# Hymba decoder step on one core: tiles 6 and 7 of the PEER layer gather u and v rows side by side

## The chip, the cores and the metric

The kernel runs on one core of a Trainium2 chip. The metric is the device time of one execution in microseconds; 3248.42 us is the median of three runs of the kernel before, which lie between 3223.76 and 3261.47 us.

## What is computed

One step of a hybrid decoder layer on 1056 tokens (1024 of a prompt, 8 x 4 sampled ones) of width 1024: an RMSNorm, a token mixer (windowed attention, gated linear attention, retention), a second RMSNorm, a PEER feed-forward layer, a final RMSNorm. The change lies in the PEER layer. It picks, for each token, 8 x 16 = 128 of 16384 experts, each of which is one row of `u_tab` and one of `v_tab` (1024 floats each):

```python
eidx = ...            # (tokens, 128): the chosen experts of each token
gate = softmax(...)   # (tokens, 128)
u = take(u_tab, eidx); v = take(v_tab, eidx)
pre = einsum('td,ted->te', xb, u)
act = gelu(pre, approximate=False) * gate
y   = x + einsum('te,ted->td', act, v)
```

## The kernel before

The tokens are cut into nine tiles of 128 rows (tile 8 has the 32 sampled tokens). The mixer runs over groups of tiles (0; 1, 2; 3, 4; 5, 8; 6, 7). Behind a tile's mixer its experts are selected on VectorE (the select ends with L710, which writes the expert numbers `ei`), and its PEER layer is done in one of two ways.

**Dense**, for tiles 2 to 5 together (512 tokens, `dense()`). All 16384 experts are gone through in 128 blocks of 128. The gates have been scattered into a dense matrix `gsd` in HBM, from which SP loads 2 MB pieces `Gt`. For block e, `up(e)` loads 512 KB of `in_uT` and 512 KB of `in_v_tab` on SP's queue into `raw` (four buffers), splits each into a high part on ScalarE (`uh`, `vh`, L981) and a low part on GpSimd (`ul`, `vl`, L982), and makes 24 matmuls of 128x512 into one PSUM bank `pre` (L1008): hh with uh, hl with uh, hh with ul. `hh` and `hl` are the high and low part of the four tiles' normed rows and are made once at the start. Then ScalarE takes the Gelu in place (L1009), VectorE multiplies by `Gt` (L1012), and the result is split into `ah` (ScalarE) and `al` (VectorE, L982). For each four blocks, `down` makes 8 groups of 12 matmuls into `out` banks (L1024), each of which VectorE adds to `oT` (L1028). At the end the four tiles are transposed back, normed and stored (L1053, L884).

**Gather**, for tiles 0, 1, 8, 6, 7 in this order (`gather()`). For each of the 128 expert columns GpSimd starts an indirect DMA that brings 128 rows of `u_tab`, one for each token, 512 KB, into one of six buffers `g` (L915). VectorE multiplies the buffer with the normed rows h2 and sums along the row in one instruction (L917, an STT below, with a short read of the accumulator behind it). After all 128 columns one Gelu (L919) and one multiply by the gates follow, and a second round of 128 indirect DMAs brings rows of `v_tab` (L930), which VectorE scales and adds to `gacc` (L932). `final` (L882 to L885) norms and stores the tile. For tiles 6 and 7 (`PSG`), h2 and then the sum lie one after the other in one PSUM tile `gacc` of two banks; PSUM's other banks are three of `pre` and three of `out`.

The order of each engine's instructions is fixed when the program is built, by a scheduler that goes by priorities: the dense path stands above the gathers, and the gathers come in where they fit. Each engine then works strictly in this order, so an instruction that waits holds up all behind it.

## Time and profile before

| | us | share of the span |
|---|---|---|
| median of three runs | 3248.42 | |
| the profiled execution, whole | 3220.93 | |
| its span, first to last instruction | 3219.0 | |
| TensorE busy | 2883.6 | 90% |
| VectorE busy | 2379.4 | 74% |
| GpSimd busy | 1897.8 | 59% |
| ScalarE busy | 1182.8 | 37% |
| moved by DMA | 980.51 MB, 305 GB/s | |

The time of all runs is the device time of one execution; the profile is of one more execution, whose span leaves out some 2 us around the program. Busy time is a mean over very different stretches: the mixer until about 1700 us, and behind it the dense path with the gathers of tiles 6 and 7 beside it. So it is read stretch by stretch. A wait is put down in the trace to the instruction or the DMA that ended it. A matmul's time as listed overlaps the next one's; the number of matmuls in a stretch gives their pace.

### The profile page before, as it was taken

The page shows a single profiled execution, that of the slowest core. Times are in us where ns is not written, and L with a number is a line of the kernel's source. Part 1 is how long each engine was busy: PE and PEld are TensorE (multiplying, and loading weights), DVE is VectorE, ACT ScalarE, POOL GpSimd, SP SyncE. Part 2 cuts the span into 40 slices and gives each one's busy share as a digit, 9 for nine tenths or more (in the row PEclk, how much of TensorE's full clock was granted, in tenths as well). Part 3 has the DMA queues.
Part 4 walks back from the last instruction along what each step waited for, and adds up shares of the span by engine and source line. Part 5 has one row for each costly group of instructions (what it writes and reads, how often), then busy time and mean ns, then how long its engine had stood idle before and what let it go on. Part 6 is the DMA issues. An engine that isn't in the chain of part 4 may idle for free. (4 is left out here: it accounts for less than half of the span.)

```text
span 3219.0 us, 41048 instructions
## 1 busy us (share of the span) xinstructions
PE 2883.6 (90%) x13566; PEld 2318.1 (72%) x13566; DVE 2379.4 (74%) x5398; ACT 1182.8 (37%) x2478; POOL 1897.8 (59%) x1447
## 2 busy tenths in 40 slices
PE   6887999996999899986764699999999999999997
PEld 5675777774786567775653578888888888888886
DVE  0375777999799967989989866667776676666673
ACT  1211213322575266776673322232323223222331
POOL 0026655655445434435554777777777888777782
PEclk9798889998899999978866899999999999999998
DMA  6379898999898988979898899999999999999982
GB/s 229 127 256 362 321 339 321 358 337 347 290 355 321 337 314 305 340 272 350 275 324 245 277 316 317 307 320 323 321 325 312 316 316 333 317 317 311 318 326 86
DMA packets 421541, 980.51 MB, mean 305 GB/s; under 512 B 163841, under 2 KB 193042, under 8 KB 421330
## 3 DMA queue, kind: packets, MB, share of 16 engines
q0 software_dynamic: 159808, 580.62, 49.5%
q1 hardware_dynamic: 261522, 397.28, 38.1%
q8 instruction: 107, 1.75, 0.2%
q14 instruction: 104, 0.85, 0.1%
HBM read 925.91 MB, written 51.45 MB: 304 GB/s over the span
## 5 line engine op out<-in xcount | busy, mean ns | idle before, releaser
L915 POOL DMA_INDIRECT g<-in_u_tab,ei x512 | 566.1, 1106 | 464.5 <-DVE g L917 187.1
L930 POOL DMA_INDIRECT g<-in_v_tab,ei x512 | 569.8, 1113 | 435.3 <-DVE gacc L932 136.1
L917 DVE SCALAR_TENSOR_TENSOR g<-g,gacc 128x1024 f32<-128x1024 f32 x544 | 654.0, 1216 | 133.3 <-DMA g<-in_u_tab,ei 125.0
L932 DVE SCALAR_TENSOR_TENSOR gacc<-g,pre,gacc 128x1024 f32<-128x1024 f32 x544 | 697.5, 1282 | 54.4 <-DMA g<-in_v_tab,ei 51.0
L1024 PE MATMUL out<-ah,vh 128*128 128x512 f32 x1024 | 385.4, 391 | 42.5 <-ACT vh L981 42.4
L1024 PE MATMUL out<-ah,vl 128*128 128x512 f32 x1024 | 392.8, 390 | 6.7 <-POOL vl L982 6.7
L1024 PE MATMUL out<-al,vh 128*128 128x512 f32 x1024 | 396.8, 391 | 0.3
L982 POOL TENSOR_TENSOR ul<-raw,uh 128x1024 fp32r<-128x1024 f32 x128 | 308.0, 2407 | 46.0 <-ACT uh L981 39.8
L982 POOL TENSOR_TENSOR vl<-raw,vh 128x1024 fp32r<-128x1024 f32 x128 | 306.8, 2413 | 10.5 <-ACT vh L981 9.2
L1028 DVE TENSOR_TENSOR oT<-oT,out 128x512 f32<-128x512 f32 x248 | 166.5, 684 | 144.5 <-PE out L1024 143.8
L1008 PE MATMUL pre<-hh,uh 128*128 128x512 f32 x1024 | 258.5, 394 | 16.2 <-DVE al L982 15.0
L1008 PE MATMUL pre<-hh,ul 128*128 128x512 f32 x1024 | 257.7, 394 | 12.6 <-POOL ul L982 12.6
L630 PE MATMUL pj<-hT,w 128*128 128x256 f32 (+2 forms) x1280 | 258.2, 352 | 4.6 <-ACT hT L261 2.8
L1008 PE MATMUL pre<-hl,uh 128*128 128x512 f32 x1024 | 258.3, 389 | 0.0
L1024 PEld LDWEIGHTS out<-ah,vh 128*128 128x128 f32 x1024 | 192.9, 189 | 83.8 <-ACT vh L981 42.8
L963 PE MATMUL sct<-o,o 128*128 128x128 f32 x1024 | 200.2, 334 | 58.7 <-ACT st L964 19.8
L981 ACT ACTIVATE uh<-raw 128x1024 fp32r<-128x1024 f32 x128 | 135.4, 1058 | 311.0 <-DMA raw<-in_uT 306.0
L1009 ACT ACTIVATE pre<-pre 128x512 f32<-128x512 f32 x128 | 74.5, 582 | 476.0 <-PE pre L1008 475.8
L963 PEld LDWEIGHTS sct<-o,o 128*128 128x128 f32 x1024 | 166.7, 229 | 99.7 <-ACT st L964 34.9
L1008 PEld LDWEIGHTS pre<-hh,uh 128*128 128x128 f32 x1024 | 194.4, 190 | 58.5 <-DVE al L982 15.4
L1008 PEld LDWEIGHTS pre<-hh,ul 128*128 128x128 f32 x1024 | 193.0, 190 | 57.8 <-POOL ul L982 18.0
L630 PEld LDWEIGHTS pj<-hT,w 128*128 128x128 f32 x1280 | 213.1, 197 | 28.6 <-issue 4.6
(293 smaller groups left out, 4874.6 us busy)
## 6 DMA issues: line engine op xcount, KB each, us to landing
raw<-in_uT SPq DMA_DIRECT2D x128, 512.0 KB, 4.5
raw<-in_v_tab SPq DMA_DIRECT2D x128, 512.0 KB, 5.2
w<-in_w_pqT SPq DMA_DIRECT2D x80, 512.0 KB, 6.4
gsd<-st SPq DMA_DIRECT2D x64, 512.0 KB, 6.4
Gt<-gsd SPq DMA_DIRECT2D x16, 2048.0 KB, 22.5
w<-in_w_inT SPq DMA_DIRECT2D x60, 512.0 KB, 6.7
w<-in_w_nat SPq DMA_DIRECT2D x60, 512.0 KB, 5.4
w<-in_w_outc SPq DMA_DIRECT2D x40, 512.0 KB, 7.1
```

The costliest lines, as they stand in the source:

```text
L630: PE.matmul(p[:, :T], w[:, kt, :], h2T[:, kt], start=kt == 0, stop=kt == 7)
L915: G.indirect_dma_start(out=g, out_offset=None, in_=I["u_tab"], in_offset=bass.IndirectOffsetOnAxis(ap=idx[:, e:e + 1], axis=0))
L917: V.scalar_tensor_tensor(g, g, 1.0, h2, op0=OP.mult, op1=OP.mult, accum_out=pre[:, e:e + 1])
L930: G.indirect_dma_start(out=g, out_offset=None, in_=I["v_tab"], in_offset=bass.IndirectOffsetOnAxis(ap=idx[:, e:e + 1], axis=0))
L932: V.scalar_tensor_tensor(acc, g, act[:, e:e + 1], acc, op0=OP.mult, op1=OP.add)
L963: PE.matmul(p[:, k * 128:(k + 1) * 128], o2[:, k % 2], o1, start=True, stop=True)
L981: S.activation(hi, x, AF.Copy)
L982: eng.tensor_tensor(lo, x, f(hi), op=OP.subtract)
L1008: PE.matmul(p, w[:, kt], x[:, kt], start=kt + n == 0, stop=kt == 7 and n == 2)
L1009: S.activation(p, p, AF.Gelu)
L1024: PE.matmul(p, w[:, ds], x, start=j + n == 0, stop=j == EG - 1 and n == 2)
L1028: V.tensor_tensor(oT[:, dt], oT[:, dt], p, op=OP.add)
```

## The change

Tiles 6 and 7 get a function of their own, `gather_rows()`. A new input `uv_tab` holds each expert's row of `u_tab` and its row of `v_tab` side by side, 8 KB. For each expert column one indirect DMA brings 128 such rows, 1 MB, into one of three buffers `g2` (8 KB a partition each; before there were six of 4 KB). VectorE forms the sum with h2 on the left half, ScalarE takes the Gelu of this one column and multiplies it by the gate (two instructions of 128x1), and VectorE adds the scaled right half to `gacc`. So there are 256 indirect DMAs for the two tiles instead of 512, and one pass instead of two. h2 and the sum lie in PSUM at the same time (`gh2`, `gacc`, two banks each); for this `pre` and `out` get two banks each instead of three. The pool `gat` of the other gathers is closed with the mixer's pools, and the gathers of tiles 0, 1 and 8 are issued ahead of that; `hl` and the `g2` buffers lie in space that `gat` had.

```diff
--- before.py
+++ after.py
@@ -140,7 +140,7 @@
     mctx = ExitStack()
     con = ctx.enter_context(tc.tile_pool(name="con", bufs=1))
     dr = ctx.enter_context(tc.tile_pool(name="dr", bufs=1, space=DRAM))
-    gat = ctx.enter_context(tc.tile_pool(name="gat", bufs=1))
+    gat = mctx.enter_context(tc.tile_pool(name="gat", bufs=1))
     t4p = {k: mctx.enter_context(tc.tile_pool(name="t_" + k, bufs=1)) for k in ("at", "kv", "nb")}
     big = mctx.enter_context(tc.tile_pool(name="big", bufs=1))
     wp = mctx.enter_context(tc.tile_pool(name="wp", bufs=1))
@@ -886,7 +886,6 @@
 
     def gather(t, ei, gate):
         r0, n = rows(t)
-        inps = t in PSG
         R = 128 // n
         ncol, idx, gt = 128 // R, ei, gate.rearrange("p h k -> p (h k)")
 
@@ -894,7 +893,7 @@
             return gat.tile([128, D], F32, name="g", bufs=GB)
 
         def wide():
-            return gps[0].tile([128, D], F32, name="gacc", bufs=1) if inps else gat.tile([128, D], F32, name="gacc", bufs=1)
+            return gat.tile([128, D], F32, name="gacc", bufs=1)
 
         if R > 1:
             idx = con.tile([128, ncol], I32, name="eip")
@@ -904,27 +903,20 @@
                 G.dma_start(gp[q * n:(q + 1) * n], gt[:n, q * ncol:(q + 1) * ncol])
             gt = gp
         h2 = wide()
-        x = gtile() if inps else h2
         for q in range(R):
-            G.dma_start(x[q * n:(q + 1) * n], h2d[r0:r0 + n])
-        if inps:
-            S.activation(h2, x, AF.Copy)
-        pre = gat.tile([128, 128], F32, name="pre", bufs=1)
+            G.dma_start(h2[q * n:(q + 1) * n], h2d[r0:r0 + n])
+        act = gat.tile([128, 128], F32, name="pre", bufs=1)
         for e in range(ncol):
             g = gtile()
             G.indirect_dma_start(out=g, out_offset=None, in_=I["u_tab"],
                                  in_offset=bass.IndirectOffsetOnAxis(ap=idx[:, e:e + 1], axis=0))
-            V.scalar_tensor_tensor(g, g, 1.0, h2, op0=OP.mult, op1=OP.mult, accum_out=pre[:, e:e + 1])
-        act = pre
-        S.activation(act[:, :ncol], pre[:, :ncol], AF.Gelu)
+            V.scalar_tensor_tensor(g, g, 1.0, h2, op0=OP.mult, op1=OP.mult, accum_out=act[:, e:e + 1])
+        S.activation(act[:, :ncol], act[:, :ncol], AF.Gelu)
         V.tensor_tensor(act[:, :ncol], act[:, :ncol], gt, op=OP.mult)
         acc = wide()
         if R > 1:
             G.memset(acc, 0.0)
-        x = gtile() if inps else acc
-        G.dma_start(x[:n], x1d[r0:r0 + n])
-        if inps:
-            S.activation(acc, x, AF.Copy)
+        G.dma_start(acc[:n], x1d[r0:r0 + n])
         for e in range(ncol):
             g = gtile()
             G.indirect_dma_start(out=g, out_offset=None, in_=I["v_tab"],
@@ -935,6 +927,32 @@
             G.dma_start(g[:n], acc[q * n:(q + 1) * n])
             V.tensor_tensor(acc[:n], acc[:n], g[:n], op=OP.add)
         final(acc[:n], n, r0, gtile(), G)
+
+    def gather_rows(t, ei, gate):
+        r0, n = rows(t)
+        gt = gate.rearrange("p h k -> p (h k)")
+
+        def gtile():
+            return g2[0].tile([128, 2 * D], F32, name="g2", bufs=GB // 2)
+
+        h2 = gps[0].tile([128, D], F32, name="gh2", bufs=1)
+        acc = gps[0].tile([128, D], F32, name="gacc", bufs=1)
+        x = gtile()
+        G.dma_start(x[:, :D], h2d[r0:r0 + n])
+        G.dma_start(x[:, D:], x1d[r0:r0 + n])
+        S.activation(h2, x[:, :D], AF.Copy)
+        S.activation(acc, x[:, D:], AF.Copy)
+        act = g2[0].tile([128, 128], F32, name="pre2", bufs=2)
+        for e in range(128):
+            g = gtile()
+            a = act[:, e:e + 1]
+            G.indirect_dma_start(out=g, out_offset=None, in_=I["uv_tab"],
+                                 in_offset=bass.IndirectOffsetOnAxis(ap=ei[:, e:e + 1], axis=0))
+            V.scalar_tensor_tensor(g[:, :D], g[:, :D], 1.0, h2, op0=OP.mult, op1=OP.mult, accum_out=a)
+            S.activation(a, a, AF.Gelu)
+            S.activation(a, a, AF.Copy, scale=gt[:, e:e + 1])
+            V.scalar_tensor_tensor(acc, g[:, D:], a, acc, op0=OP.mult, op1=OP.add)
+        final(acc, n, r0, gtile()[:, :D], G)
 
     def scatter(t, gfl, gate):
         n = rows(t)[1]
@@ -964,9 +982,10 @@
                 S.activation(st[:, :, q:q + 4], p.rearrange("p (k i) -> p i k", k=4), AF.Copy)
             SP.dma_start(gsd[(doff[t] + b) // TB], st.rearrange("p i t -> p (i t)"))
 
-    gps = []
+    gps, g2 = [], []
 
     def dense():
+        g2.append(ctx.enter_context(tc.tile_pool(name="g2", bufs=1, reuse_waits="tile")))
         dp, da, dg, dv, do = (ctx.enter_context(tc.tile_pool(name="d%d" % k, bufs=1, reuse_waits="tile"))
                               for k in range(5))
         dps = ctx.enter_context(tc.tile_pool(name="dps", bufs=1, space=PSUM, reuse_waits="tile"))
@@ -1002,7 +1021,7 @@
             vh = dv.tile([128, D], F32R, name="vh", bufs=EG)
             vl = dv.tile([128, D], F32R, name="vl", bufs=EG)
             split(v, vh, vl, G)
-            p = dps.tile([128, TD], F32, name="pre", bufs=3)
+            p = dps.tile([128, TD], F32, name="pre", bufs=2)
             for n, (w, x) in enumerate(((uh, hh), (uh, hl), (ul, hh))):
                 for kt in range(8):
                     PE.matmul(p, w[:, kt], x[:, kt], start=kt + n == 0, stop=kt == 7 and n == 2)
@@ -1017,7 +1036,7 @@
 
         def down(first, grp):
             for dt in range(8):
-                p = dps.tile([128, TD], F32, name="out", bufs=3)
+                p = dps.tile([128, TD], F32, name="out", bufs=2)
                 ds = slice(dt * 128, (dt + 1) * 128)
                 for j, (vh, vl, ah, al) in enumerate(grp):
                     for n, (w, x) in enumerate(((vh, ah), (vh, al), (vl, ah))):
@@ -1041,7 +1060,7 @@
             SP.dma_start(x1[:n], x1d[r0:r0 + n])
             ps = []
             for half in range(2):
-                p = dps.tile([128, 512], F32, name="out", bufs=3)
+                p = dps.tile([128, 512], F32, name="out", bufs=2)
                 for k in range(4):
                     PE.transpose(p[:n, k * 128:(k + 1) * 128], oT[:, half * 4 + k, doff[t]:doff[t] + n], ident)
                 ps.append(p)
@@ -1065,12 +1084,17 @@
         with tc.high_priority(ATTP):
             attention(gs[i])
         outproj(gs[i])
+    with tc.high_priority(-2 * LOW):
+        for q in peer_q:
+            if q[0] not in PSG:
+                gather(*q)
     mctx.close()
     with tc.high_priority(DP):
         dense()
     with tc.high_priority(-2 * LOW):
         for q in peer_q:
-            gather(*q)
+            if q[0] in PSG:
+                gather_rows(*q)
     ctx.close()
 
 
@@ -1102,6 +1126,7 @@
     a["g_final"] = c(i["g_final"])
     a["u_tab"] = c(i["u_tab"][0])
     a["v_tab"] = c(i["v_tab"][0])
+    a["uv_tab"] = c(np.concatenate([a["u_tab"], a["v_tab"]], 1))
     a["uT"] = c(a["u_tab"].reshape(128, 128, 8, 128).transpose(0, 3, 2, 1)).reshape(128, 128, 1024)
     kv = i["cache_kv_win"][0]
     a["kcT"] = c(kv[:, :, 0].transpose(2, 3, 0, 1).reshape(4, 128, 8, 256).transpose(1, 0, 2, 3))
```

Where the dense path begins, the order of instructions changes. On VectorE, this stood before at the end of tile 7's select (`tk` are its work tiles, L710 its end, L917 are STTs of tile 6's u rows, ten of which stand ahead of L710; the `hl` splits and the first blocks' ops stand further up, in the mixer):

```order
L693 TENSOR_TENSOR tk<-iota_107,ab 128x2048
L917 SCALAR_TENSOR_TENSOR g,pre<-g,gacc 128x1024 x2
L695 TENSOR_TENSOR tk<-tk 128x2048
L917 SCALAR_TENSOR_TENSOR g,pre<-g,gacc 128x1024 x2
L697 TENSOR_TENSOR tk<-tk 128x8x128
L917 SCALAR_TENSOR_TENSOR g,pre<-g,gacc 128x1024
L697 TENSOR_TENSOR tk<-tk 128x8x64
L917 SCALAR_TENSOR_TENSOR g,pre<-g,gacc 128x1024
L697 TENSOR_TENSOR tk<-tk 128x8x32
L698 TENSOR_TENSOR tk<-tk 128x128
L710 SCALAR_TENSOR_TENSOR ei<-tk 128x128
L917 SCALAR_TENSOR_TENSOR g,pre<-g,gacc 128x1024
```

And this after, where L951 and L954 are the two halves of an expert column of tile 6:

```order
L695 TENSOR_TENSOR tk<-tk 128x2048
L697 TENSOR_TENSOR tk<-tk 128x8x128
L697 TENSOR_TENSOR tk<-tk 128x8x64
L884 SCALAR_TENSOR_TENSOR g<-gacc,rsg,g 32x1024
L697 TENSOR_TENSOR tk<-tk 128x8x32
L698 TENSOR_TENSOR tk<-tk 128x128
L710 SCALAR_TENSOR_TENSOR ei<-tk 128x128
L1001 TENSOR_TENSOR hl<-raw,hh 128x512 x4
L951 SCALAR_TENSOR_TENSOR g_23186,pre_23185<-g_23186,gh_23178 128x1024
L1001 TENSOR_TENSOR hl<-raw,hh 128x512
L954 SCALAR_TENSOR_TENSOR gacc<-g_23186,pre_23185,gacc 128x1024
L951 SCALAR_TENSOR_TENSOR g_23192,pre_23185<-g_23192,gh_23178 128x1024
```

The `hl` splits, without which no dense matmul can start, have moved behind the select. On GpSimd, this stood before from tile 1's last v gathers on (L930) to the loads of tile 8's gates and indexes (L904, L903):

```order
L930 DMA g<-in_v_tab,ei 128x1024 x19
L982 TENSOR_TENSOR ul<-raw,uh 128x1024
L930 DMA g<-in_v_tab,ei 128x1024
L243 TENSOR_TENSOR rsb<-ssb,mhalf 128x1
L982 TENSOR_TENSOR ul<-raw,uh 128x1024
L930 DMA g<-in_v_tab,ei 128x1024 x5
L243 TENSOR_TENSOR rsb<-ssb,mhalf 128x1
L982 TENSOR_TENSOR ul<-raw,uh 128x1024
L930 DMA g<-in_v_tab,ei 128x1024 x8
L904 DMA gatep<-gate_10382 32x32 x4
L930 DMA g<-in_v_tab,ei 128x1024 x4
L903 DMA eip<-ei 32x32 x4
```

And this after, from tile 8's last v gathers (L922) to tile 6 (L949):

```order
L927 DMA g<-gacc 32x1024 x3
L882 DMA g<-in_g_final 128x1024
L243 TENSOR_TENSOR rsg<-ssg,mhalf 32x1
L885 DMA out_y<-g 32x1024
L941 DMA g_23180<-h2d 128x1024
L942 DMA g_23180<-x1d 128x1024
L949 DMA g_23186<-in_uv_tab,ei 128x2048
L949 DMA g_23192<-in_uv_tab,ei 128x2048
L949 DMA g_23198<-in_uv_tab,ei 128x2048
L949 DMA g_23204<-in_uv_tab,ei 128x2048
L949 DMA g_23210<-in_uv_tab,ei 128x2048
L1001 TENSOR_TENSOR ul<-raw,uh 128x1024
```

The first low splits `ul` of the dense path stood among tile 1's gathers; now the first one stands behind all of tile 8 and behind the first five gathers of tile 6. In the middle of the dense stretch, VectorE's queue reads before (tile 7's v rows):

```order
L1012 TENSOR_TENSOR pre<-pre,Gt 128x512
L982 TENSOR_TENSOR al<-pre,ah 128x512
L932 SCALAR_TENSOR_TENSOR gacc<-g,pre,gacc 128x1024 x6
L1012 TENSOR_TENSOR pre<-pre,Gt 128x512
L982 TENSOR_TENSOR al<-pre,ah 128x512
L1012 TENSOR_TENSOR pre<-pre,Gt 128x512
L932 SCALAR_TENSOR_TENSOR gacc<-g,pre,gacc 128x1024
L982 TENSOR_TENSOR al<-pre,ah 128x512
L932 SCALAR_TENSOR_TENSOR gacc<-g,pre,gacc 128x1024
L1028 TENSOR_TENSOR oT<-oT,out 128x512 x3
```

And after (tile 7 too):

```order
L1031 TENSOR_TENSOR pre<-pre,Gt 128x512
L951 SCALAR_TENSOR_TENSOR g_23918,pre_23185<-g_23918,gh_23178 128x1024
L1001 TENSOR_TENSOR al<-pre,ah 128x512
L954 SCALAR_TENSOR_TENSOR gacc<-g_23918,pre_23185,gacc 128x1024
L1047 TENSOR_TENSOR oT<-oT,out 128x512
L951 SCALAR_TENSOR_TENSOR g_23924,pre_23185<-g_23924,gh_23178 128x1024
L1047 TENSOR_TENSOR oT<-oT,out 128x512
L954 SCALAR_TENSOR_TENSOR gacc<-g_23924,pre_23185,gacc 128x1024
L1031 TENSOR_TENSOR pre<-pre,Gt 128x512
L951 SCALAR_TENSOR_TENSOR g_23930,pre_23185<-g_23930,gh_23178 128x1024
L1047 TENSOR_TENSOR oT<-oT,out 128x512
L954 SCALAR_TENSOR_TENSOR gacc<-g_23930,pre_23185,gacc 128x1024
```

Each expert column now has its two halves close to each other, and between the two ScalarE has to do its two small instructions. On 44 of the 256 columns the right half stands directly behind its left half.

## Rows read from the trace of the kernel before

**Rows 1.** The page: the span, and the software DMA queue's line

```profile
span 3219.0 us, 41048 instructions
...
q0 software_dynamic: 159808, 580.62, 49.5%
```

**Rows 2.** Stretches: length, busy PE, PEld, DVE, ACT, POOL, clock, DMA, GB/s

```profile
1500.00:1600.00 100.00, 63.86 (x305) 54.25 (x304) 95.15 (x250) 50.07 (x119) 49.34 (x41) 0.81 0.85 311
...
1700.00:1800.00 100.00, 34.11 (x120) 26.38 (x120) 91.63 (x237) 27.81 (x36) 45.98 (x40) 0.62 0.83 242
...
1850.00:3100.00 1250.00, 1236.46 (x5419) 1017.62 (x5418) 858.48 (x1155) 354.95 (x456) 991.81 (x703) 1.00 0.96 319
```

**Rows 3.** Timeline of PE, 1700:1800: start, duration, operation, [idle before]

```profile
1706.78 3.64 PE L1008 MATMUL pre<-hh,uh 128*128 128x512 f32 x8
...
1739.96 3.78 PE L1008 MATMUL pre<-hh,uh 128*128 128x512 f32 x8 [15.00 <-DVE al L982]
...
1790.05 0.80 PE L1024 MATMUL out<-ah,vh 128*128 128x512 f32 x1 [42.35 <-ACT vh L981]
...
1799.10 0.80 PE L1024 MATMUL out<-ah,vl 128*128 128x512 f32 x1 [6.12 <-POOL vl L982]
```

**Rows 4.** Timeline of VectorE in 1725:1740 and 1760:1815

```profile
1735.09 1.90 DVE L1012 TENSOR_TENSOR pre<-pre,Gt 128x512 f32<-128x512 f32 x3 [5.27 <-DMA Gt<-gsd]
...
1805.05 4.84 DVE L697 TENSOR_TENSOR tk<-tk 128x512 bf16<-128x512 bf16 x1
...
1811.59 0.29 DVE L710 SCALAR_TENSOR_TENSOR ei<-tk 128x128 int32<-128x128 f32 x1
```

**Rows 5.** Groups of 1850:3100, shapes apart: busy us, mean ns, idle before

```profile
L932 DVE SCALAR_TENSOR_TENSOR gacc<-g,pre,gacc 128x1024 f32<-128x1024 f32 x241 | 309.5, 1284 | 46.1 <-DMA g<-in_v_tab,ei 43.5
L982 POOL TENSOR_TENSOR ul<-raw,uh 128x1024 fp32r<-128x1024 f32 x114 | 274.4, 2409 | 39.5 <-ACT uh L981 33.5 <-PE pre L1008 2.5 <-PE out L1024 1.9
L917 DVE SCALAR_TENSOR_TENSOR g<-g,gacc 128x1024 f32<-128x1024 f32 x229 | 274.2, 1216 | 79.7 <-DMA g<-in_u_tab,ei 78.1 <-ACT gacc L911 0.8
...
L915 POOL DMA_INDIRECT g<-in_u_tab,ei x226 | 214.2, 948 | 97.9 <-DVE g L917 47.6 <-issue 38.6 <-DVE pre L1012 2.6
...
L1028 DVE TENSOR_TENSOR oT<-oT,out 128x512 f32<-128x512 f32 x227 | 152.4, 684 | 118.7 <-PE out L1024 118.1
...
L917 DVE DVE_READ_ACCUMULATOR g<-g,gacc 128x1 f32 x229 | 18.8, 82 | 0.0
...
L919 ACT ACTIVATE pre<-pre 128x128 f32<-128x128 f32 x2 | 0.6, 310 | 6.1 <-DVE g L917 6.1
...
L248 ACT ACTIVATION_READ_ACCUMULATOR g<-gacc 128x1 f32 x1 | 0.2, 193 | 0.0
```

**Rows 6.** Waits of 1850:3100: us in total, times, longest

```profile
ACT pre L1009 <- PE pre L1008: 452.6, 91, 10.5
...
DVE g L917 <- DMA g<-in_u_tab,ei: 78.1, 52, 6.8
POOL g L930 <- DVE gacc L932: 72.7, 56, 6.2
...
PE pre L1008 <- POOL ul L982: 12.6, 11, 2.8
```

**Rows 7.** DMA of 1850:3100: the software queue; landings of L915

```profile
q0 software_dynamic: 68515, 249.47, 53.8%
...
DMA to landing us min/median/max: 4.6/6.2/12.4
```

**Rows 8.** Timeline near the end

```profile
3132.74 1.29 DVE L932 SCALAR_TENSOR_TENSOR gacc<-g,pre,gacc 128x1024 f32<-128x1024 f32 x1 [1.16 <-DMA g<-in_v_tab,ei]
...
3163.08 0.60 ACT L981 ACTIVATE ah<-pre 128x512 fp32r<-128x512 f32 x1 [0.77 <-DVE pre L1012]
...
3163.71 0.69 DVE L982 TENSOR_TENSOR al<-pre,ah 128x512 fp32r<-128x512 f32 x1 [0.66 <-ACT ah L981]
...
3194.55 0.69 DVE L1028 TENSOR_TENSOR oT<-oT,out 128x512 f32<-128x512 f32 x1 [2.04 <-PE out L1024]
```

## The prediction

> **What bounds the kernel now.** I read the execution as a whole first. Its span is 3219.0 us [rows 1]; with what lies around it the profiled run took 3220.93 us, 27 us below the median of 3248.42, so the sum is made against 3219 and its difference is put on the median. Then I read stretches. From 1850 to 3100 us the dense path runs, and tiles 6 and 7 are gathered beside it. There PE is busy for 1236 of 1250 us at clock 1.00, the DMA engines for 0.96 of the time, POOL for 992 us and DVE for 858 [rows 2]. So this stretch is bound by PE, with the DMA close behind it. PE makes 5419 matmuls in 1236.5 us, 0.228 us each, and 48 for an expert block (24 in `up`, 24 in `down`): 10.95 us a block, 1402 us for 128.
>
> PE does not run like this at once. Its first dense matmuls stand at 1706.78; then it waits 15.0 us for `al` and 42.35 us for `vh`, and it flows only from 1799.10 [rows 3]. By then the `up` half of four blocks is done, 4 x 24 x 0.228 = 21.9 us. Flowing from 1799.1 with 1402 - 21.9 us to do would end at 3179; the last `out` is added at 3194.55 [rows 8], so about 16 us are lost on the way, most of them the waits of PE for `ul` (12.6 us [rows 6]) and others like it.
>
> The gathers are off the path now: the last v row is taken in at 3132.74, and PE has some 60 us more to do [rows 8].
>
> **What the change removes.** 256 of 512 gather issues of tiles 6 and 7. One takes 0.948 us on POOL plus 0.25 us of issuing before the next [rows 5], so about 307 us of POOL go. The bytes and the DVE work stay. POOL's relief is worth nothing by itself: PE waits 12.6 us for POOL in the whole stretch [rows 6], and this is the most that could come back. PE's work hides POOL; without that cover the 307 us would count.
>
> **The start of the dense path.** In the order of DVE, before, the eight `hl` splits, the first four blocks' ops and ten of tile 6's STTs stand ahead of the end of tile 7's select (L710, 1811.59 [rows 4]). After, L710 stands ahead of `hl`, so no dense matmul can start before the select ends, and on POOL the first `ul` stands behind tile 8's whole gather. (On SBUF `hl` takes part of the space of the old `g` buffers.) What leaves DVE's queue ahead of L710: 8 `hl` and 4 x 2 ops of 128x512 at about 0.68 us = 10.9, the wait for `Gt` 5.3, ten STTs of 1.216 + 0.082 = 13.0, and the stretch of one select op that took 4.84 us [rows 4, 5] and its like, about 7. Sum 36 us, so L710 would end at about 1775.5. Behind it: four `hl` (2.7), then `hl` 4 to 7 through the freed `raw` buffers, `uT` and its split. I give these 13 us by two landings of 4.6 to 6.2 us [rows 7] and an ACT split. The first matmul stands at about 1788.5, with all 1402 us to do and the same 16 lost: 3206.5 instead of 3194.55, **+12 us**. The bounds: if L710 ends another 15 us earlier (the DVE is less than full only where others hold it), -3; if nothing of DVE's work was on that path, L710 stays at 1811.6 and the sum is +48.
>
> **The pace of the gathers.** After, two gathers of 1 MB must be done for each block, one per 10.95 / 2 = 5.48 us, from three buffers instead of six half as large. A buffer may then be held for 3 x 5.48 = 16.4 us. It is held for:
> - the issue, 0.95 + about 0.25: 1.2 us [rows 5].
> - the landing. Half a megabyte takes 4.6 us at least, 6.2 in the median, 12.4 at most [rows 7]. No row shows a whole one. From below: one packet of the software queue takes 0.495 x 3219 x 16 / 159808 = 0.16 us of an engine [rows 1], 128 more rows on 16 engines are 8 packets each, +1.3 us: 7.5. From above: twice the median, 12.4. The queue has only 0.538 of the engines' time here [rows 7], which makes of 1.3 us 2.4: 8.6, and I take this.
> - DVE: the u half 1.216 + 0.082, the v half 1.284 [rows 5], and between them the new round trip to ACT, Gelu and Copy of 128x1. The nearest rows of ACT are 0.19 (128x1, reading the accumulator) and 0.31 (128x128) [rows 5]; a hand-over between the engines takes 0.03 (`ah` ends at 3163.68, `al` starts at 3163.71 [rows 8]). So 0.45 to 0.7 us; I take 0.57. Sum 3.15.
> - standing in queues. On POOL, `ul` and `vl` take 2.41 us each [rows 5], and in the new order up to four of them stand between two gathers, 9.6 us in a row about once in four blocks: over the 43.8 us of four blocks that, with the four single `ul`, makes a mean wait of (9.6 x 9.6 + 4 x 2.41 x 2.41) / 2 / 43.8 = 1.3 us. On DVE an STT stands behind ops of 0.68 and behind other STTs, about 1.4 us for both halves. On ACT 46 of the 256 pairs stand right behind the Gelu of a block's `pre`, before which ACT waits 452.6 us for PE in 91 waits of 5 us [rows 6]; 46 / 256 x 5 = 0.9. Sum 3.6; bounds 0 and about 5.
>
> Together 1.2 + 8.6 + 3.15 + 3.6 = 16.55 us, 5.52 a gather: just what PE allows. With the bounds it is 4.0 to 7.3. A loop with no slack doesn't hold its mean: a landing twice as long as the median has only two other buffers behind it where it had five, the order of POOL ties each gather to the splits that PE needs, and DVE, which took the ops in turn, now stands still for 0.57 us in the 44 places of its order where the v half is right behind its u half. Before, DVE already waited 78.1 us for u rows and POOL 72.7 us for buffers [rows 6], with the finer grain. I take 5.7 us, nearer to the sum than to the upper bound: 256 x (5.7 - 5.48) = **+56 us**.
>
> The Trainium skill speaks for the change here: DMA: Bandwidth & Descriptors (Anatomy of one DMA, and the rule under Bandwidth) gives a DMA 2.0 us plus its bytes at 436 GB/s and wants at least 1 MiB in one. By it a whole gather would land in about 4.4 us, an estimate for an idle queue, and the loop would keep pace, with +12 us for the whole. The trace has 6.2 us for half of that size beside a queue at 0.96, so the measurement decides.
>
> **The PSUM banks.** `pre` and `out` go from three banks to two. In the order before, five groups of 12 `out` matmuls stand in a row; after, they come in pairs with 11 matmuls of `pre` between (2.5 us). A group takes 2.7 us, and DVE's add 0.68 us. With two banks, DVE may be 2.7 us late before PE waits, and one round trip or one STT pair (3.15) is more than that. I cost this at 0 while DVE is on time, and up to 0.5 us in each of 256 groups at worst, +128, which lies in the range. The work that covers it is the matmul group of the other bank.
>
> **The end.** The gathers now end with the last four `vl`, not 60 us earlier; the tail after PE (3194.55 to 3219) is the same: 0 to +1.
>
> Sum: 3219 + 12 + 56 = 3287 us of span, +68; on the median 3248 + 68 = about 3315.
>
> **The rivals.**
> - **PE stays the bound.** The landing is 7.5 us or the queues cost half: the loop needs 5.0 us, the order waits for PE, and only the start counts: 3248 + 12 = 3260 (-15 to +30). For it: my own sum comes out just at PE's pace. Against: four stations of the loop now lie one behind the other.
> - **PE falls out of its full clock.** If gathers take 6.2 us, the loop alone costs 256 x 0.7 = +180 us, and PE waits in every block. Where PE waited in the mixer, the granted clock, a mean of its two levels of 1.2 and 2.4 GHz, was lower: 0.81 from 1500 to 1600 us and 0.62 from 1700 to 1800 [rows 2]. At 0.85 in the dense stretch a block takes 12.9 us, 128 x 1.95 = +250 us, so about 3500. For it: landings of up to 12.4 us. Against: the bytes in flight are the same three megabytes.
> - **Faster.** The mixer's tail, relieved of dense work, ends so early that PE flows sooner than now. Equal is a first matmul at 1799.1 - 21.9 = 1777; a gain of over 1% (32 us) asks for 1745, so for L710 at 1732. DVE is 92% busy from 1700 to 1800 [rows 2], and only 36 us of it go. With the lost 16 us gone too, and L710 at 1755, it would be 3248 - 25 = about 3223. Against: DVE's remaining work.
> - **The change doesn't do what it says**, that is, each 8 KB row still moves as two packets and nothing is saved in the queue: this is in the landing that I took, and changes nothing else.
>
> **How the numbers follow.** Gather loop just too slow (+30 to +180): 0.43. PE stays the bound: 0.36. Clock or landing far worse (above +180): 0.14. Faster by over 1%: 0.07. One per cent is about what a measurement of this kernel can tell from no change (its runs lie between 3224 and 3261). So faster 0.07, same 0.36, slower 0.57. The likeliest is the first, 3315 us, with its own range 3278 to 3428. The range of the forecast is 3225 to 3430: it leaves out the fast rival and a part of the worst.
>
> **What would show it.** Right: first dense matmul at 1780 to 1795 with tile 7's L710 just ahead; in the dense stretch, PE below 96% with waits on `ul`, `al` or `out`, DVE waiting for gathered rows at L951 and for ACT at L954, POOL waiting for g2 buffers at L949; landings of 8 to 9 us. Wrong: PE at 99% and a pace of 10.95 us a block (first rival); a clock below 0.95 there (second); a first matmul before 1760 (third).

## The result, and the profile after

The changed kernel is slower. In one comparison it took 3287.62 us (median of four runs) against 3239.90 us of the kernel before, a ratio of 1.0151 (95% interval 1.0102 to 1.0200). A second program with the same order of instructions (e5 below) gave 1.0103 (1.0068 to 1.0138), so 1.0 to 1.5% is what the change costs, some 33 to 49 us. 3315 was forecast, +68; the direction and half to three quarters of the size came out, but not from the terms as they were forecast.

The page of the changed kernel: the span, then busy time, share and instructions of each engine, and the software DMA queue (packets, MB, share of 16 engines).

```profile
span 3279.9 us, 40955 instructions
...
PE 2906.2 (89%) x13566; PEld 2329.9 (71%) x13566; DVE 2358.4 (72%) x5396; ACT 1283.5 (39%) x2986; POOL 1655.0 (50%) x1191
...
q0 software_dynamic: 122944, 580.61, 47.9%
```

POOL's busy time fell by 243 us (256 issues of 0.95 us), and bought nothing. The queue moved the same megabytes in 122944 packets instead of 159808 [rows 1].

Stretches of the changed kernel (columns as in [rows 2]):

```profile
1700.00:1800.00 100.00, 8.81 (x35) 7.39 (x34) 87.56 (x218) 28.85 (x54) 41.77 (x37) 0.50 0.86 260
...
1900.00:3150.00 1250.00, 1220.23 (x5317) 997.51 (x5316) 810.37 (x1103) 442.03 (x888) 744.81 (x449) 1.00 0.88 301
```

Two places lose. From 1700 to 1800 PE stands still but for 9 us, where it did 34 us of work before. In the dense stretch PE is idle for 30 of 1250 us instead of 13.5 and makes 102 matmuls fewer, some 23 us of its work, at clock 1.00 (2.4 GHz, the upper level) as before. The DMA share is down from 0.96 to 0.88.

The start, in the timelines of PE, VectorE and ScalarE of the changed kernel (start, duration, operation, idle before and its releaser):

```profile
1712.01 2.07 PE L981 MATMUL sct<-o,o 128*128 128x128 f32 x8 [1.18 <-ACT st L982]
1806.30 3.78 PE L1027 MATMUL pre<-hh,uh 128*128 128x512 f32 x8 [92.21 <-ACT uh L1000]
...
1786.00 0.29 DVE L710 SCALAR_TENSOR_TENSOR ei<-tk 128x128 int32<-128x128 f32 x1
1786.21 1.28 DVE L1001 TENSOR_TENSOR hl<-raw,hh 128x512 fp32r<-128x512 f32 x2
1793.49 1.29 DVE L1001 TENSOR_TENSOR hl<-raw,hh 128x512 fp32r<-128x512 f32 x2 [6.00 <-ACT hh L1000]
...
1791.89 1.03 ACT L943 ACTIVATE gh<-g 128x1024 f32<-128x1024 f32 x1 [11.08 <-DMA g<-h2d]
...
1805.10 0.20 ACT L952 ACTIVATE pre<-pre 128x1 f32<-128x1 f32 x1 [2.80 <-DVE g L951]
```

PE ends the scatter at 1714.1 and waits 92 us for the first dense block. The `hl` splits begin right behind tile 7's select, as the order said. Two of them then stand 6 us longer, because ScalarE, which makes their `hh`, waits in order for the load of tile 6's h2 first.

The waits of the changed kernel from 1900 to 3150 us (total, times, longest), and the durations of the new instructions there:

```profile
ACT pre L952 <- DVE g L951: 411.7, 169, 6.9
POOL ul L1001 <- ACT uh L1000: 292.7, 45, 16.6
...
POOL g L949 <- DVE gacc L954: 147.2, 71, 5.0
DVE pre L1031 <- ACT pre L1028: 116.0, 53, 6.5
DVE g L951 <- DMA g<-in_uv_tab,ei: 105.8, 68, 4.5
...
DVE gacc L954 <- ACT pre L953: 92.5, 60, 6.1
...
PE pre L1027 <- DVE al L1001: 18.6, 18, 2.2
...
PE pre L1027 <- ACT uh L1000: 7.4, 10, 1.3
```

```profile
L953 ACT ACTIVATE pre<-pre,gate 128x1 f32<-128x1 f32 x220 | 63.0, 289 | 4.8
L952 ACT ACTIVATE pre<-pre 128x1 f32<-128x1 f32 x219 | 43.7, 200 | 411.8 <-DVE g L951 411.7
```

All the engines around PE wait a lot for each other now; PE itself waits for `al`, which holds a `pre` bank until VectorE has read it, and for `uh`. Before, 12.6 of its 13.5 us of idle time were for `ul` [rows 2, rows 6].

The last scatter matmuls of the kernel before, and the last add of the changed kernel:

```profile
1705.93 1.20 PE L963 MATMUL sct<-o,o 128*128 128x128 f32 x4 [0.39 <-DVE o L956]
```

```profile
3250.41 0.69 DVE L1047 TENSOR_TENSOR oT<-oT,out 128x512 f32<-128x512 f32 x1 [2.03 <-PE out L1043]
```

Where the 61 us between the two profiled executions lie, in parts that can be added. The profiled execution of before lies 19 us under the median of its runs (3220.93 against 3239.90), that of the change 5 us under (3282.27 against 3287.62), so some 14 of the 61 us may be spread between executions:
- 7.0 us ahead of the last scatter matmul (1707.1 before, 1714.1 after). There the engines do the same work but for the last gathers, and over all the executions of this study this point lies between 1705 and 1728. This is spread, and the rest is counted from there.
- The start. Before, PE flows from 1799.1 with 21.9 us done, as if it had begun at 1777.2, 70.1 us behind the scatter; after, 92.2 us behind: **+22**.
- The dense path from there to the end of the last add: 1418.0 before, 1444.8 after: **+27**.
- Behind the last add: 23.8 before, 28.8 after: **+5**. The last instructions stand as before; the 5 us lie behind the last store, and were not traced further.

### The profile page after: what moved, and what is told of

The parts are those of the page before. It is cut to its first block, busy times and chain, and to the rows that moved or that the text cites. A ratio compares the mean times of both kernels' runs of the same rounds, so it can differ in the third digit from the quotient of the medians.

```text
span 3279.9 us, 40955 instructions
## 1 busy us (share of the span) xinstructions
PE 2906.2 (89%) x13566; PEld 2329.9 (71%) x13566; DVE 2358.4 (72%) x5396; ACT 1283.5 (39%) x2986; POOL 1655.0 (50%) x1191
## 3 DMA queue, kind: packets, MB, share of 16 engines
q0 software_dynamic: 122944, 580.61, 47.9%
## 5 line engine op out<-in xcount | busy, mean ns | idle before, releaser
L911 POOL DMA_INDIRECT g<-in_u_tab,ei x256 | 314.7, 1229 | 364.0 <-DVE g L913 144.6
L922 POOL DMA_INDIRECT g<-in_v_tab,ei x256 | 329.9, 1289 | 312.6 <-DVE gacc L924 56.2
L954 DVE SCALAR_TENSOR_TENSOR gacc<-g,pre,gacc 128x1024 f32<-128x1024 f32 x256 | 328.9, 1285 | 101.8 <-ACT pre L953 101.1
L951 DVE SCALAR_TENSOR_TENSOR g<-g,gh 128x1024 f32<-128x1024 f32 x256 | 311.1, 1215 | 120.0 <-DMA g<-in_uv_tab,ei 119.5
L1043 PE MATMUL out<-ah,vh 128*128 128x512 f32 x1024 | 393.2, 390 | 4.1 <-ACT vh L1000 3.1
L913 DVE SCALAR_TENSOR_TENSOR g<-g,gacc 128x1024 f32<-128x1024 f32 x288 | 347.3, 1215 | 45.4 <-DMA g<-in_u_tab,ei 42.2
L949 POOL DMA_INDIRECT g<-in_uv_tab,ei x256 | 243.4, 951 | 260.2 <-DVE gacc L954 187.7
L1027 PE MATMUL pre<-hh,uh 128*128 128x512 f32 x1024 | 267.4, 400 | 120.0 <-ACT uh L1000 99.6
L1027 PE MATMUL pre<-hl,uh 128*128 128x512 f32 x1024 | 265.2, 391 | 0.0
L952 ACT ACTIVATE pre<-pre 128x1 f32<-128x1 f32 x256 | 51.1, 200 | 474.0 <-DVE g L951 474.0
```

The costliest lines, as they stand in the source:

```text
L911: G.indirect_dma_start(out=g, out_offset=None, in_=I["u_tab"], in_offset=bass.IndirectOffsetOnAxis(ap=idx[:, e:e + 1], axis=0))
L913: V.scalar_tensor_tensor(g, g, 1.0, h2, op0=OP.mult, op1=OP.mult, accum_out=act[:, e:e + 1])
L922: G.indirect_dma_start(out=g, out_offset=None, in_=I["v_tab"], in_offset=bass.IndirectOffsetOnAxis(ap=idx[:, e:e + 1], axis=0))
L949: G.indirect_dma_start(out=g, out_offset=None, in_=I["uv_tab"], in_offset=bass.IndirectOffsetOnAxis(ap=ei[:, e:e + 1], axis=0))
L951: V.scalar_tensor_tensor(g[:, :D], g[:, :D], 1.0, h2, op0=OP.mult, op1=OP.mult, accum_out=a)
L954: V.scalar_tensor_tensor(acc, g[:, D:], a, acc, op0=OP.mult, op1=OP.add)
```

## The experiments

Each kernel's profiled execution is measured by the same two lengths, taken from the timelines: "dense" from where PE flows (less 0.228 us for each `up` matmul that it has done by then) to the end of the last add, and "whole" from the end of the last scatter matmul to there. The last column is PE's busy time in the 1000 us from 2000 to 3000. Each length is of one execution, and these lie between 19 us under (before) and 19 us above (e9) the median of their kernel, so a difference of some 10 us between two lengths says little.

| kernel | ratio to before, 95% interval | whole | dense | PE busy of 1000 us |
|---|---|---|---|---|
| before | 1 | 1488 | 1418 | 991 |
| the change | 1.0151 (1.0102 to 1.0200) | 1537 | 1445 | 975 |
| e5 (same order as the change) | 1.0103 (1.0068 to 1.0138) | 1540 | 1449 | 976 |
| e1: start moved up | 1.0107 (1.0075 to 1.0139) | 1523 | 1446 | 980 |
| e2: no gather columns of tiles 6, 7 | one run, 3235.0 us | 1487 | 1399 | 1000 |
| e3: before, pre 2, out 2 banks | 1.0154 (1.0115 to 1.0193) | 1550 | 1481 | 960 |
| e11: before, pre 2 | 1.0067 (1.0044 to 1.0090) | 1514 | 1445 | 976 |
| e12: before, out 2 | 1.0203 (1.0154 to 1.0252) | 1560 | 1490 | 950 |
| e6: the change, two 4 KB DMAs | 1.0204 (1.0151 to 1.0258) | 1564 | 1473 | 965 |
| e9: the change, 3 and 3 banks, no sum | 1.0071 (1.0041 to 1.0101) | 1527 | 1435 | 985 |
| e10: e9 with the start moved up | 1.0071 (1.0043 to 1.0099) | 1487 | 1413 | 992 |
| e4c: the change, Gt in 1 MB pieces | 1.0496 (1.0453 to 1.0540) | – | – | 930 |
| e7: e4c, h2 in SBUF, 3 and 3 banks | 1.0695 (1.0643 to 1.0747) | – | – | 895 |
| e8: e7 with the start moved up | 1.0680 (1.0618 to 1.0741) | – | – | 895 |

**e1: is the start late because of the space?**

```diff
-        dp, da, dg, dv, do = (ctx.enter_context(...
+        do, dp, da, dg, dv = (ctx.enter_context(...
```

> The changed kernel with one thing moved: the pool of oT (16 KB, not written before the first down) is opened right behind the g2 buffers, so that it, and no longer hl, lies over the end of the old gather buffers. Theory (the start is late because hl waits for space that tile 8's gather holds): the order has the hl splits ahead of both selects again, the first dense matmul comes before 1750 us, three or four up halves are done before 1800, and the span falls by 20 to 35 us from 3280, to about 3250; the dense stretch keeps its pace of about 11.2 us a block. Rival (the start is late because VectorE is full there, whatever the order): span within 8 us of 3280.

```profile
1704.82 2.81 PE L1027 MATMUL pre<-hh,uh 128*128 128x512 f32 x8
...
1792.54 1.22 PE L1043 MATMUL out<-ah,vh 128*128 128x512 f32 x2 [75.82 <-ACT ah L1000]
```

In this timeline of PE the first block comes at 1704.82, 101 us earlier: the place of `hl` held it. But only two `up` halves are done before PE waits 76 us for `ah`: the multiply by `Gt` ahead of it stands in VectorE's queue behind tile 7's select (L710 at 1784.24, the multiply at 1791.17). The whole is 14 us shorter, the dense part as it was. The median gain (1.0107 against 1.0151 and 1.0103) is no larger than the spread of the changed kernel itself. So the space is the cause of the late first block. Giving it back is worth some 14 of the 22 us in this trace, which is that of e1's fastest execution; in the times it does not show.

**e2: what do the gathers cost?**

```diff
-        for e in range(128):
+        for e in range(0):
```

> The changed kernel without the 128 expert columns of tiles 6 and 7 (their part of the PEER sum is left out; h2, x1 and the final norm stay). Theory (the gather loop costs the dense stretch its 27 us, two banks each of pre and out cost nothing): PE waits under 8 us between 1900 and 3100, 10.9 to 10.95 us a block, the last add about 1400 to 1410 us after the first dense matmul instead of 1444. Rival (two banks are the cost): PE still waits 25 to 30 us in that stretch, and the distance stays above 1430.

```profile
2000.00:3000.00 1000.00, 1000.00 (x4414) 828.03 (x4413) 250.73 (x368) 289.61 (x368) 438.03 (x184) 1.00 0.44 120
```

PE never waits in these 1000 us (columns as in [rows 2]), with two banks each, and the dense part takes 1399 us: the floor. So two banks cost nothing by themselves, and all that is above 1399 comes with the gathers.

**e3, e11, e12: what are the banks worth to the old gather?**

```diff
-            p = dps.tile([128, TD], F32, name="pre", bufs=3)
+            p = dps.tile([128, TD], F32, name="pre", bufs=2)
...
-                p = dps.tile([128, TD], F32, name="out", bufs=3)
+                p = dps.tile([128, TD], F32, name="out", bufs=2)
```

(e3 both, e11 the first, e12 the second.)

> The kernel before with two banks of pre and two of out instead of three, and nothing else changed (two banks are left free). Theory (banks cost nothing): within 0.4% of before, PE waits 10 to 20 us between 1850 and 3100 as before (13). Rival (banks cost the 27 us of the dense stretch): 0.7 to 1% slower, PE waits 30 to 45 us there, before matmuls of pre or out that follow an add or a Gelu. Third possibility, as forecast at worst: up to 0.5 us in each of 256 groups, 4% slower.

> The kernel before with two banks of pre, three of out. Theory (pre is the bank that ties PE to the chain of Gelu, Gt, ah and al on ScalarE and VectorE, where the gather's STTs stand between): most of the 1.5% that two and two banks cost, so 0.9 to 1.6% slower than before. Rival (out, which waits for one add alone, is the one): within 0.4%.

> The kernel before with three banks of pre, two of out. Theory (pre is the one): within 0.4% of before. Rival (out is the one): 0.9 to 1.6% slower. If both this and the run with two banks of pre cost 0.5 to 1%, the two add up.

Stretch and PE's waits of e12, 2000 to 3000 us:

```profile
2000.00:3000.00 1000.00, 949.55 (x4067) 768.42 (x4066) 686.22 (x914) 269.70 (x348) 777.64 (x564) 0.98 0.94 316
```

```profile
PE pre L1008 <- POOL ul L982: 21.3, 13, 3.7
PE out L1024 <- ACT ah L981: 9.0, 8, 2.0
PE pre L1008 <- ACT uh L981: 7.4, 7, 1.6
PE out L1024 <- DVE oT L1028: 6.6, 6, 1.5
```

With the old gather, two and two banks cost 63 us of the dense path, and in the times as much as the whole change (1.0154 against 1.0151). That was held to be free. And it is the bank of `out`, not that of `pre`, that matters most: 72 us against 27, or 2.0% against 0.7%. Little of it is listed as a wait for a bank (6.6 us for the add); most is waits for `ul`, `ah` and `uh`. With two `out` banks, the `down` matmuls can't run ahead of VectorE's adds, the order puts `pre` matmuls in between, and lateness anywhere in the chain reaches PE; this is read from the order and the waits and was not tested by itself. The idle time isn't all of it: behind these waits the granted clock is 0.98 instead of 1.00, so PE takes 949.55 / 4067 = 0.233 us a matmul instead of 0.228, some 20 us more in the 1000. The two costs don't add up (e3 is below e12); each kernel has its own order of instructions, and this part is not explained further.

**e5: the round trip to ScalarE.**

```diff
-            V.scalar_tensor_tensor(acc, g[:, D:], a, acc, ...)
+            if e:
+                V.scalar_tensor_tensor(acc, pg[:, D:], pa, acc, ...)
+            pg, pa = g, a
```

> The changed kernel with the v half of each expert column put behind the u half of the next one, in the program's text, so that the Gelu and the gate of a column have a whole column's time; a buffer is then held about one column longer. Theory (three buffers bind: the loop has no slack to hold a buffer longer): slower than the changed kernel by 1.5 to 8%, VectorE's wait for gathered rows at the u half grows from 106 us to over 250. Rival (the round trip from VectorE to ScalarE and back binds, 92 us of waits at the v half): these waits fall below 30 us and the kernel gains 10 to 27 us on the changed one.

It tests neither. The scheduler put the v halves back where they were, and VectorE's queue holds the same operations in the same order as in the changed kernel, from its first row to its last. It stands here as a second measurement of the change. Whether the round trip costs anything stays open.

**e6: one DMA of 8 KB rows, or two of 4 KB?**

```diff
-            G.indirect_dma_start(out=g, ..., in_=I["uv_tab"], ...)
+            G.indirect_dma_start(out=g[:, :D], ..., in_=I["u_tab"], ...)
+            G.indirect_dma_start(out=g[:, D:], ..., in_=I["v_tab"], ...)
```

> The changed kernel with two indirect DMAs of 4 KB rows per expert column, one into each half of the same buffer, instead of one of 8 KB rows: 512 issues again. Theory (the size of the DMA is not what counts; POOL and the queue have slack): within 0.5% of the changed kernel, landings of the second half 0.5 to 1.5 us later than the 7.9 us of the whole. Rival (8 KB rows lighten the queue: 8 KB packets, DMA busy 0.88 instead of 0.96): DMA share back at 0.93 or more and 0.5 to 2% slower than the changed kernel.

```profile
2000.00:3000.00 1000.00, 964.80 (x4176) 787.00 (x4175) 652.79 (x889) 357.70 (x715) 766.74 (x543) 0.99 0.93 306
```

PE's waits in the same 1000 us:

```profile
PE out L1045 <- ACT ah L1002: 20.8, 11, 2.6
...
PE pre L1029 <- POOL ul L1003: 0.6, 1, 0.6
```

The DMA share is 0.93, where the changed kernel has 0.88 for the same bytes, and the dense path takes 1473 us instead of 1445. So the single DMA counts, against the theory, for some 28 us. Two things change in e6 at once, the size and the number of issues: POOL is busy for 767 of 1000 us instead of 590. PE waits for POOL's `ul` only 0.6 us there, which speaks for the size, but no run parts the two. The changed kernel's own rows, 1900 to 3150 us: the software queue, and the landings of L949:

```profile
q0 software_dynamic: 31977, 230.77, 48.5%
```

```profile
DMA to landing us min/median/max: 5.3/7.9/11.8
```

That is 7.2 KB a packet in the mean, and 7.9 us for what took 6.2 us at half the size [rows 7]. The Trainium skill's rule in DMA: Bandwidth & Descriptors (Bandwidth), to make DMAs of 1 MiB and more, speaks for this part of the change, and the trace agrees: twice the bytes landed in 7.9 us instead of 6.2.

**e4c, e7, e8: the banks back, with h2 in SBUF.** To find 4 KB for h2, `Gt` was cut into pieces of half the size; e4c is the control for it.

```diff
-EC = 8
+EC = 4
-GTB = 2
+GTB = 3
...
-        h2 = gps[0].tile([128, D], F32, name="gh2", bufs=1)
+        h2 = g2[0].tile([128, D], F32, name="gh2", bufs=1)
```

> Control: the changed kernel with Gt in pieces of 1 MB (three buffers of 8 KB) and nothing else. Expected by all theories: within 0.4% of the changed kernel, 1.1 to 1.9% above before; the start as late as in the changed kernel (first dense matmul about 1800 to 1810). If it gains more than 0.6% on the changed kernel, the pieces of Gt explain a part of what the three-bank kernel shows.

> The changed kernel with its three banks of pre and three of out back: h2 of tiles 6 and 7 lies in SBUF (4 KB beside the g2 buffers), for which Gt comes in pieces of 1 MB (three buffers of 8 KB instead of two of 16). The 4 KB also push hl off the end of the old gather buffers, so its order has the dense start as early as before. Theory (two things cost the time: the start, and two banks that leave PE no lead over VectorE): the dense stretch runs at 11.05 us a block or less, PE's waits for al behind pre are gone, first dense matmul before 1730; the whole within 0.4% of before. Rival (the gather loop itself costs the dense stretch, whatever the banks): as e1, 0.8 to 1.2% above before, PE still waits 25 us in 2000 to 3000.

> The three-bank kernel with the pool of oT opened right behind the g2 buffers, as in e1, so that hl and hh lie over later-freed or earlier-freed mixer buffers. Theory (the order of the start, not the place, sets the time once hl is off the gather buffers): within 0.5% of the three-bank kernel. A first matmul earlier than there by 10 us or more, with no gain at the end, would say that DVE's queue holds the flow back until the selects are done.

The control alone costs 3.5% more, so e7 and e8 say nothing on the banks; what they ran into stands in the last section.

**e9, e10: the banks back without that.**

```diff
-        acc = gps[0].tile([128, D], F32, name="gacc", bufs=1)
+        acc = h2
-            V.scalar_tensor_tensor(acc, g[:, D:], a, acc, ...)
+            V.scalar_tensor_tensor(g[:, D:], g[:, D:], a, acc, ...)
```

(and three banks each of `pre` and `out`; e10 with e1's line too)

> The changed kernel with three banks each of pre and out. For the room in PSUM, the sum of tiles 6 and 7 is left out: the v half, still one STT of 128x1024 with one operand in PSUM (h2), writes its product back into the gathered buffer, and h2 stands for the sum at the end. DMAs, the two STTs, Gelu and gate of each column stay. Theory (two banks cost the dense stretch its time, the gather in one pass doesn't): from the first dense matmul to the last add 1405 to 1420 us instead of 1444, first matmul still at about 1806; 0.5 to 1.0% above before. Rival (the loop over three buffers costs it, whatever the banks): 1437 us or more, 1.2 to 1.7% above before.

> The kernel of the run before it (three banks each, the sum of tiles 6 and 7 left out) with the pool of oT opened right behind the g2 buffers, as in e1. Theory (start and banks are all of the loss): within 0.4% of before, last add at 3190 to 3205. Rival (gather loop): 0.8 to 1.2% above before.

Stretch of e9, then stretch and VectorE's end of e10:

```profile
2000.00:3000.00 1000.00, 985.36 (x4305) 809.61 (x4303) 646.91 (x880) 355.67 (x713) 599.43 (x359) 0.99 0.89 301
```

```profile
2000.00:3000.00 1000.00, 991.56 (x4345) 816.71 (x4344) 660.26 (x898) 354.01 (x716) 598.85 (x362) 1.00 0.90 306
```

```profile
3206.49 0.69 DVE L1046 TENSOR_TENSOR oT<-oT,out 128x512 f32<-128x512 f32 x1 [0.80 <-PE out L1042]
...
3225.52 1.28 DVE L953 SCALAR_TENSOR_TENSOR g<-g,pre,gh 128x1024 f32<-128x1024 f32 x1
```

The v halves of the changed kernel, of e9 and of e10 (shortest, median and longest in ns, first and last start):

```profile
L954 DVE SCALAR_TENSOR_TENSOR gacc<-g,pre,gacc x256: 1274/1287/1291, 1798.2 to 3226.8; 128x1024 f32<-128x1024 f32 x128
```

```profile
L953 DVE SCALAR_TENSOR_TENSOR g<-g,pre,gh x256: 1270/1280/1283, 1806.4 to 3236.1; 128x1024 f32<-128x1024 f32 x128
```

```profile
L953 DVE SCALAR_TENSOR_TENSOR g<-g,pre,gh x256: 1270/1280/1284, 1804.8 to 3225.5; 128x1024 f32<-128x1024 f32 x128
```

With banks and start both given back (e10), PE is busy for 992 of 1000 us and the whole is 1487 us, the value of before. Leaving out the sum hardly changes the v half itself (1280 ns instead of 1287). In the dense path the banks are worth 33 us (e10 against e1) or 10 (e9 against the change), but the traced execution of e9 lies 19 us above its median and that of e1 13 below; e9's 1435 stands beside its rival's 1437 and not in the theory's 1405 to 1420. In the last column they are worth 12 and 10 of 1000 us, in the times 0.4% (1.0071 against 1.0107) and 0.3 to 0.8% (1.0071 against 1.0103 and 1.0151), with intervals that touch or overlap. But e10 is still 0.7% slower than before. The gathers now end last: the last v half ends 20 us behind the last add, and the whole program 40 us behind it instead of 24. Three banks hardly made the gathers faster: from the first to the last v half a column takes 5.60 us in the changed kernel, 5.61 in e9 and 5.57 in e10. In e10 PE is ahead of them, with 1413 / 256 = 5.52. So the rival of the gather loop is right in part, at the end of the program and not in the stretch.

No kernel here beats the one before. Its dense path lies 19 us above the floor of e2, so in this stretch there was hardly anything to gain.

## Why the prediction was right, and where it was not

- **PE bounds the dense path, and POOL's relief is worth nothing.** Right. POOL is busy for 243 us less, and the time rises.
- **The start, +12.** Right in its cause (`hl` behind the select and behind tile 8's buffers, shown by e1), too small: +22. Counted from the last scatter matmul, L710 came 3.5 us later than forecast (71.9 against 68.4 us). The step from there to the first matmul took 20.3 us instead of 13. VectorE stood 6 us of it because ScalarE waited for tile 6's h2, which stands in its queue between the `hh` splits; and the first `uh` stood there behind the Gelu of a gather column, which waited 2.80 us for its u half. For the start, what a wait holds up behind it was asked of VectorE only.
- **The pace of the gathers, 5.7 us, +56.** The number was close: 220 gathers in 1250 us are 5.68 us each. The term was too large, +27, because PE's own 16 us of losses were counted beside it, and they lie in the same waits: 256 x 5.64 us is the whole dense path of 1445. The cause is shown in part only. It was put down to the time that three buffers are held, and the waits that were named for this came: VectorE for rows 105.8 us, POOL for buffers 147.2. The pieces of the sum were fair (landing 7.9 for 8.6 us, the two ScalarE instructions 0.20 + 0.29 us where 0.4 to 0.6 was taken; its lower bound adds up to 3.9, not 4.0). With three banks the gathers keep nearly the same pace, 5.57 us in e10, still above PE's 5.48; but there PE runs at 992 of 1000 us, and the gathers cost time only behind the last add. So their pace need not be PE's, as the forecast took it to be; with the late start (e9) PE's path still has their pace, 1435 / 256 = 5.61 us. What sets this pace, the buffers or the places of the halves in VectorE's order, no run separates.
- **The PSUM banks, 0.** This is the step that failed. With the same two and two banks, the dense path of the old loop is 1481 us and that of the new one 1445: the new gather is 37 us better, and 28 of these go with the single DMA of 8 KB rows (e6). The two banks cost the old loop 63 us, 0.25 us for each of the 256 groups, where the forecast had 0 and at worst 0.5. Added in this order, +63 and -37 make the +27. In the other order the new loop with three banks costs +17 (e9), or -5 with the start moved up (e10), and the two banks +10 or +33. In either order the banks are not 0 and the loop is far from +56, so that the sum came near was luck in good part. What misled it was to ask whether VectorE's add is late for a bank, 2.7 us of cover. As e12's waits read, the bank is a lead that absorbs lateness from the whole chain, and its loss shows as waits for `ul` and `ah`.
- **The end, 0 to +1.** +5, behind the last store.
- **The rivals.** That PE stays the bound with only the start to pay for (3260) is not what happened, though the time alone would lie in its range, up to 3290: the dense path lost 27 us. The clock stayed at 1.00 in the stretch, so the second didn't come; the third neither. That 8 KB rows would still move as two packets was wrong: the queue has 36864 packets fewer, and 256 gathers of 128 rows are 32768 of them.
- **What would show it.** The signs came out between right and wrong. PE is 97.6% busy in the dense stretch (1220.23 of 1250 us), not below 96% and not at 99%. The first dense matmul stands at 1806.30 instead of 1780 to 1795, of which 7 us are spread. PE waits for `al`, as was said, but hardly for the `out` banks, and for `uh` instead of `ul`.

## What to carry to other kernels

Ask of every buffer that a change takes away what lateness it had been absorbing, and measure it alone: run the old kernel with the new kernel's banks. Here that one run (e3) is as slow as the change itself. A faster helper gives nothing beside an engine that is 99% busy, and it can take away the slack that kept it busy. When a pool moves, look for what the scheduler can no longer start early; and where a new load feeds an in-order engine, see what stands behind it there.

## What the runs showed beside the question

**An STT with both operands in SBUF is held up by GpSimd.** With h2 in SBUF (e7) the u half's STT takes 2144 ns in the mean instead of 1215, and one of them 8.09 us, beside a run of four `vl` of GpSimd. Group of 2000 to 3000 us, and the timeline, of e7:

```profile
L951 DVE SCALAR_TENSOR_TENSOR g<-g,gh 128x1024 f32<-128x1024 f32 x155 | 331.9, 2144 | 47.7 <-DMA g<-in_uv_tab,ei 47.5
```

```profile
2245.53 9.44 POOL L1001 TENSOR_TENSOR vl<-raw,vh 128x1024 fp32r<-128x1024 f32 x4
2247.97 8.09 DVE L951 SCALAR_TENSOR_TENSOR g<-g,gh 128x1024 f32<-128x1024 f32 x1 [2.07 <-DMA g<-in_uv_tab,ei]
```

The Trainium skill says so (SBUF — State Buffer, SBUF: two separate sides): of a VectorE instruction with two SBUF inputs and a GpSimd one that reads SBUF, the one that starts first has their common port for its whole length, and the other is blocked. The trace agrees, and here it is not one instruction that the STT waits for but the whole run: the four `vl` end at 2254.97, the STT 1.1 us later at 2256.06. With h2 and the sum in PSUM, as in the changed kernel, the STT keeps its 1215 ns; that is what the two banks were given for.

**A load of many short rows blocks its queue.** Each `Gt` load has 8192 rows, of 256 bytes, or of 128 in e4c. SP's timeline of e4c and of the changed kernel:

```profile
2229.11 0.43 SPq L1013 DMA_DIRECT2D Gt<-gsd  x1
2231.10 15.45 SPq L1016 DMA_DIRECT2D raw<-in_uT  x1
```

```profile
2237.77 0.38 SPq L1013 DMA_DIRECT2D Gt<-gsd  x1
2238.26 16.59 SPq L1020 DMA_DIRECT2D raw<-in_v_tab  x1
```

The issue of the next load takes 15 to 19 us behind a load of the changed kernel and 13 to 18 behind one of e4c (8 to 10 in e2, where the DMA engines are busy for 0.44 of the time), so here it goes more with the number of rows, which is the same, than with the bytes; another number of rows was not run. At half the size it comes twice as often. Stretch and PE's waits of e4c, 2000 to 3000 us:

```profile
2000.00:3000.00 1000.00, 930.16 (x3900) 752.50 (x3899) 596.46 (x814) 323.49 (x654) 544.83 (x330) 0.96 0.90 278
```

```profile
PE pre L1027 <- ACT uh L1000: 44.5, 17, 8.3
PE out L1043 <- DVE oT L1047: 18.6, 12, 2.6
```

PE waits 44.5 us for `uh`, where it waited 7.4, and 18.6 us for VectorE's adds, where it waited 0.7; and with the clock at 0.96 a matmul takes 0.239 us instead of 0.230. Together this is the 3.5%; the three were not tried apart.
